# Hybrid decoder layer on one core: the second parts of the first feed-forward, all by seven products

## The chip, the cores and the metric

The kernel runs on one core of a Trainium2 chip, as one program. The metric is the device time of one execution in microseconds. The kernel before took 1702.88 us, the median of three runs (1699.06 to 1704.96).

## The reference

One layer works on 1024 tokens of width 1024, in float32:

```python
h = modulate(rms_norm(x, ffn1_norm), sh1, sc1)
x = x + 0.5 * g1 * ((silu(h @ w_gate) * (h @ w_up)) @ w_down)      # first feed-forward, D_FF = 2816
h = modulate(rms_norm(x, mix_norm), sh2, sc2)
b, c, v, u = split(h @ w_in)                                       # gated convolution and state-space part
x = x + g2 * (concat(rms_norm(y_conv), rms_norm(y_ssm)) @ w_out)
h = modulate(rms_norm(x, ffn2_norm), sh3, sc3)
x = x + 0.5 * g3 * ((silu(h @ w_gate2) * (h @ w_up2)) @ w_down2)   # second feed-forward
y = rms_norm(x, final_norm)
```

The nine vectors sh, sc and g come from `silu(cond) @ w_mod + b_mod`; each of them has 1024 elements.

## The kernel before

The activations lie transposed: features on the 128 partitions, tokens along the row, in two token halves h of 512. Every product keeps its precision by splitting both operands into a high and a low part: `mm3` (line 306) is three matmuls of 128x128 by 128x512 and one tick of a clock that is counted while the program is built. A weight tile of 128x1024 goes from a raw buffer through a cast on ScalarE (high part) and a subtraction on VectorE (low part) into one of four ring buffers (`Weights.pump`). Where sums of two weight blocks are needed, a DMA from GpSimd's queue adds the second block to the raw buffer.

The 2816 inner features of a feed-forward are 11 groups of 256. The first part of a group is its gate and up projections; the second part multiplies the group's 256 activations with its rows of w_down. `seven` (line 626) and `down7` (line 699) compute a 2x2 block product with seven block products instead of eight, as in Strassen's method in Winograd's form. In `down7` the left operands are the activations A11, A12, A21, A22 of a group (token half by feature half) and their sums S1 to S4. They are stored in DRAM by `Kept` (line 477) and loaded again by `fetch` (line 687) as 128x512 tiles: a DMA on SP's queue, a cast on ScalarE, a subtraction on VectorE. A Kept object made with `all_seven` false stores only the A tiles. The sums are made by `keep_sums` and `keep_last`, with four VectorE instructions for a group.

One call of `down7` does a chunk of four groups in two passes p. A pass takes the products of `SEVEN` in their order (A11, S1, S2, S4, S3, A12, A22), each for two output blocks i of 128, into the PSUM banks B, C and A. ScalarE copies three intermediate results out of PSUM (t1, c1, u2), VectorE adds others to them and updates the residual x. The order of products is so chosen that an accumulation into bank C goes on after its copy c1.

Before, the first feed-forward does groups 1 to 4 and 5 to 8 in two chunks (`fad0`, `fad1`). Groups 0, 9 and 10 are done plainly by `last_parts` (line 1391): for each half of the outputs and each token half, 24 calls of mm3 for each of the three groups, tiles named fald. While the second pass of a chunk runs, the operands of the next are fetched, four after each product.

After the last update of a token half, `after1` (line 1312) adds its squares (ScalarE squares, GpSimd or VectorE adds) and orders the norm by clock ticks: 8 ticks later TensorE sums the squares over partitions (n2ast), 7 ticks later it spreads the root (n2abc), and from then on the eight blocks of the next activations h2 are made, one for each tick or when they are asked for. The next TensorE work, the u products, takes these blocks in order, four weight tiles for each block.

`side2` (line 1297) makes 20 elements of 128 of the modulation vectors in this stage, tiles named wm: each a DMA of 512 KB and one multiply-and-sum of 128x1024 on VectorE. One of them is written out at every fourth tick; what is left is written out when the stage ends (`while clock.side: clock.step()`). In this stage each of them carries an edge that keeps it behind the VectorE instruction written before it.

The tile framework orders the instructions of each engine when the program is built, by the order in which they were written and by its own estimate of when their operands are ready. An instruction that it takes to be ready early can be drawn forward. On the chip each engine then works through its queue in that order.

Of the kernel before, what the change touches and what calls it, by code (L numbers as in the profile page):

```python
# [13 lines left out]
F32 = mybir.dt.float32  # L14
# [3 lines left out]
ALU = mybir.AluOpType  # L18
# [3 lines left out]
P = 128  # L22
# [3 lines left out]
KT = D // P  # L26
# [9 lines left out]

CHUNKS = 2

LAST = ((0, NGRP - 2, NGRP - 1), (NGRP - 2, NGRP - 1))
J = S // TAU  # L40
# [79 lines left out]
class Weights:  # L120
# [25 lines left out]

    def seven(self, b, inner=()):
# [11 lines left out]
        self.order.extend(got[q] for q in (2, 3, 4, 1, 5, 6))  # L159

# [4 lines left out]
    def add(self, r, src):  # L165
        self.G.dma_start(out=r[:], in_=src, accum_op=ALU.add)  # L166

    def load(self, upto):
        while len(self.raws) < min(upto, len(self.srcs)):
            i = len(self.raws)  # L170
            r = self.raw_pool(i).tile([P, 1024], F32, tag="raw", name=f"raw{i}")
            src, more = self.srcs[i]
            self.SP.dma_start(r[:], src)
            if more is not None:
                self.add(r, more)
            self.raws.append(r)
# [6 lines left out]
    def pump(self):  # L183
        while self.slots and len(self.tiles) < len(self.granules):
            i = len(self.tiles)
            j, more = self.granules[i]
            self.load(j + 1)
            src = self.raws[j][:]
# [3 lines left out]
            hi, lo = w[:, 0, :], w[:, 1, :]  # L192
            self.A.copy(hi, src)
# [27 lines left out]
@with_exitstack  # L221
def hymba_layer(ctx: ExitStack, tc, x_d, xt_d, wm1_d, wmod_d, gu1_d, gs1_d, ds1_d, wl1_d, win_d, wout_d, glu_d, gu2_d, gs2_d, wd2_d, ds2_d, wl2_d, cols_d, cond_d, lam_d, bc_d, out_d):
    nc = tc.nc
# [56 lines left out]
    def stream(gu, gs, wd, ds, wl, m):  # L280


        for g in range(m):
            plain([gu[2 * g], gu[2 * g + 1]])
        for g in range(m, NGRP):
            ws.seven(gs[g - m], [wd[:, q, :] for q in range(2)] if g == 1 else ())
        for c in range(CHUNKS):
            for p in range(2):
                ws.seven(ds[c, p])
        plain([wl[i] for i in range(wl.shape[0])])  # L290

    stream(gu1_d, gs1_d, None, ds1_d, wl1_d, SEVEN_FROM[0])
    plain([win_d[i] for i in range(8)] + [glu_d] + [wout_d[i] for i in range(4)])
    stream(gu2_d, gs2_d, wd2_d, ds2_d, wl2_d, SEVEN_FROM[1])
    ws.raw_pool = lambda i: pro if i == 3 else rawp

# [390 lines left out]
    def fetch(kept, left, where, name):  # L687
# [6 lines left out]
        SP.dma_start(whole_, kept.stored(left))  # L694
        A.copy(hi, whole_)
        V.tensor_tensor(out=lo, in0=whole_, in1=hi.bitcast(F32), op=ALU.subtract)
        return hi, lo

    def down7(name, lefts, n_, then=None, first=None):

        for p in range(2):
            bank, t1, c1, u2 = {}, {}, {}, {}

            def update(i, h, half, src):
# [10 lines left out]

            for n, (left, b) in enumerate(SEVEN):
                (w,) = ws.take()
                for i in range(2):
                    opens = (b, i) not in bank
                    if opens:  # L720
                        bank[b, i] = ps(f"{name}_{p}_{i}{b}")
                    for k in range(4):
                        mm3(bank[b, i][:], w, 4 * (k // 2) + 2 * (k % 2) + i, lefts[left][k], opens and k == 0, k == 3, more=not opens)
                    if n == 0:
                        copied(t1, "B", i, "t1")
                    elif n == 1:
                        copied(c1, "C", i, "c1")
                    elif n == 2:
                        copied(u2, "B", i, "u2")
                    elif n == 3:  # L730
                        add(u2, "C", i)
                        update(i, 0, 1, u2[i])
                    elif n == 4:
                        add(c1, "B", i)
                        update(i, 1, 1, c1[i])
                    elif n == 5:
# [144 lines left out]

    kept, afs = {0: kept_for(0, 0 not in LAST[0])}, {}

# [101 lines left out]

    kept.update({g: kept_for(g, g not in LAST[0]) for g in range(1, NGRP)})
    gu_first(1)
# [369 lines left out]
    clock.period = 4.5  # L1357
    lefts = [{left: [] for left, _ in SEVEN} for _ in range(CHUNKS)]
    a_last = [{} for _ in LAST[0]]
# [6 lines left out]
    def fetch_last(left):  # L1366

        if left in ("A11", "A12", "A22"):
            i = ("A11", "A12", "A22").index(left)
            for h in range(2):  # L1370
                for fi in range(2):
                    a_last[i][fi, h] = fetch(kept[LAST[0][i]], f"A{h + 1}{fi + 1}", "A", f"fa{LAST[0][i]}l")

# [11 lines left out]
    down7("fad0", lefts[0], 0, lambda left: fetch_chunk(1, left), lambda left: load_x(range(2), (1, 3)) if left == "A12" else None)  # L1385
    down7("fad1", lefts[1], 0, fetch_last)
    clock.period = 4
    clock.side.append(side2(mod_mov, MODS[2]))
    pools["mixed"] = False

    def last_parts():
        for dh in range(2):
            wd = ws.take(3)
            for h in range(2):
                outs = [ps(f"fald{4 * dh + i}_{h}") for i in range(4)]
                for q, (w, a) in enumerate(zip(wd, a_last)):
                    for fi in range(2):
                        for i, o in enumerate(outs):
                            mm3(o[:], w, 4 * fi + i, a[fi, h], q == fi == 0, q == 2 and fi == 1)
                    if h:  # L1400
                        ws.free()
                for i, o in enumerate(outs):
                    d = 4 * dh + i
                    V.scalar_tensor_tensor(out=x[d][h], in0=o[:], scalar=gate[:, 0, d : d + 1], in1=x[d][h], op0=ALU.mult, op1=ALU.add)
                    after1(d, h)

    last_parts()
    while clock.side:
# [290 lines left out]
    HOMES = dict(A11="B", S2="A", A12="B", S3="A", S1="B", A22="A", S4="A")  # L1699
    lefts = [{left: [] for left in HOMES} for _ in range(CHUNKS)]  # L1700
    a_last = {}
# [77 lines left out]
def _arrays(i):  # L1779
# [7 lines left out]
    for n in (1, 2):  # L1787
# [5 lines left out]
        if n == 2:  # L1793
            a["wd2"] = b[0].transpose(1, 2, 0, 3).reshape(P, 2, 1024)
        b = b[list(LAST[n - 1])].transpose(3, 0, 2, 1, 4).reshape(-1, 2, P, 1024)
        a[f"wl{n}"] = b.transpose(0, 2, 1, 3)

        b = wd.reshape(NGRP, 2, P, 2, 2, 2, P)[1 : 1 + 4 * CHUNKS].reshape(CHUNKS, 2, 2, 2, P, 2, 2, 2, P)
        b = b.transpose(0, 6, 1, 4, 3, 5, 2, 7, 8)

        b = [b[:, :, :, :, q, r].reshape(CHUNKS, 2, 2, P, 512).swapaxes(2, 3).reshape(CHUNKS, 2, P, 1024) for q, r in FOUR]
        a[f"ds{n}"] = np.stack(b, axis=2)
        a[f"gu{n}"] = np.stack([g, u], axis=2).reshape(NF, P, 2, 1024)[: 2 * m]
# [21 lines left out]

_ORDER = ["x", "xt", "wm1", "wmod", "gu1", "gs1", "ds1", "wl1", "win", "wout", "glu", "gu2", "gs2", "wd2", "ds2", "wl2", "cols", "cond", "lam", "bc"]

# [16 lines left out]
```

## Time and profile before

| what | value |
|---|---|
| timed runs, median (range) | 1702.88 us (1699.06 to 1704.96) |
| profiled execution, its own time | 1695.99 us |
| span from the first to the last instruction | 1694.2 us |
| matmuls | 7545 recorded |
| first chunk, passes 1 and 2 | 480.3 to 524.2, to 562.3 us |
| second chunk | 562.3 to 638.5 us |
| plain part of three groups | 638.5 to 705.6 us |
| u products | from 705.6 us |

The profiled execution is one more execution than the timed ones and is faster than each of them; durations are read from it. PE is TensorE, DVE VectorE, ACT ScalarE, POOL GpSimd and SP the engine whose queue issues most of the DMAs. A matmul's recorded duration (389 ns) is longer than the distance between two of them, since they overlap. PEclk is the granted share of TensorE's full clock.

### The profile page before, as it was taken

The page shows a single profiled execution, that of the slowest core. Times are in us where ns is not written, and L with a number is a line of the kernel's source. Part 1 is how long each engine was busy: PE and PEld are TensorE (multiplying, and loading weights), DVE is VectorE, ACT ScalarE, POOL GpSimd, SP SyncE. Part 2 cuts the span into 40 slices and gives each one's busy share as a digit, 9 for nine tenths or more (in the row PEclk, how much of TensorE's full clock was granted, in tenths as well). Part 3 has the DMA queues.
Part 4 walks back from the last instruction along what each step waited for, and adds up shares of the span by engine and source line. Part 5 has one row for each costly group of instructions (what it writes and reads, how often), then busy time and mean ns, then how long its engine had stood idle before and what let it go on. Part 6 is the DMA issues. An engine that isn't in the chain of part 4 may idle for free.

```text
span 1694.2 us, 20669 instructions
## 1 busy us (share of the span) xinstructions
PE 1664.0 (98%) x7545; PEld 1370.0 (81%) x7545; DVE 1063.2 (63%) x1572; ACT 670.3 (40%) x983; POOL 165.2 (10%) x203
## 2 busy tenths in 40 slices
PE   8999999999999999999999999999999999999997
PEld 5887878788878888788888778888888888888887
DVE  7976676776566767735666847856555655454454
ACT  7526333333454432332214416434444444322234
POOL 1001000001001102200000121000001001000003
PEclk9999999999999999999999999999999999999999
DMA  9557897887887768235753323557787777989812
GB/s 361 177 164 187 227 265 213 219 210 200 276 275 202 209 177 291 73 101 161 209 156 113 100 99 143 132 136 222 237 234 204 221 219 219 321 272 343 255 60 100
DMA packets 128552, 338.11 MB, mean 200 GB/s; under 512 B 22337, under 2 KB 37953, under 8 KB 127426
## 3 DMA queue, kind: packets, MB, share of 16 engines
q1 hardware_dynamic: 112898, 280.16, 47.7%
q0 software_dynamic: 15552, 56.63, 19.3%
q8 instruction: 59, 0.97, 0.2%
q14 instruction: 43, 0.35, 0.1%
HBM read 252.32 MB, written 76.02 MB: 194 GB/s over the span
## 4 chain that ended last, share of the span: by engine, by line
PE 80%; DVE 8%; DMA 7%; ACT 2%; issue 1%; SPq 1%; POOL 0%; DVEq 0%; POOLq 0%; ACTq 0%
PE fald L111 4%; DMA wm<-in_wmod 3%; PE p L111 3%; PE fbd_1B L111 3%; PE fbd_0B L111 3%; PE fb10d L111 2%; PE fad_0B L111 2%; PE fad_1B L111 2%; PE wo L111 2%; PE b L111 2%; PE u L111 2%; PE fad_1C L111 1%; DMA swx<-X 1%; PE fbd_1C L111 1%; PE fbd_0C L111 1%
## 5 line engine op out<-in xcount | busy, mean ns | idle before, releaser
L111 DVE TENSOR_TENSOR w<-raw,w 128x1024 fp32r<-128x1024 f32 x239 | 292.5, 1226 | 248.3 <-ACT w L111 237.2
L111 ACT CAST w<-raw 128x1024 fp32r<-128x1024 f32 x239 | 250.9, 1051 | 305.0 <-DMA raw<-in_ds 59.4
L166 POOL DMA_DIRECT2D raw<-in_gs x76 | 66.7, 878 | 753.5 <-DVE w L111 425.9
L111 DVE CUSTOM_DVE_ANT_0 wm<-wm,cact 128x1024 f32<-128x1024 f32 x56 | 75.7, 1374 | 38.6 <-DMA wm<-in_wmod 38.6
L166 POOL DMA_DIRECT2D raw<-in_ds x32 | 28.0, 875 | 284.4 <-DVE w L111 162.5
L111 PE MATMUL p<-h,w 128*128 128x512 f32 x192 | 49.4, 407 | 1.7 <-ACT h L111 1.5
L111 PE MATMUL wo<-oa,w 128*128 128x512 f32 x192 | 46.7, 399 | 2.2 <-ACT w L111 2.2
L111 PE MATMUL wo<-ob,w 128*128 128x512 f32 x192 | 45.7, 392 | 1.1 <-ACT ob L111 0.6
L111 PE MATMUL v<-h,w 128*128 128x512 f32 x192 | 46.0, 393 | 0.0
L111 PE MATMUL c<-h,w 128*128 128x512 f32 x192 | 46.0, 393 | 0.0
L111 PEld LDWEIGHTS wo<-oa,w 128*128 128x128 f32 x192 | 36.9, 193 | 10.5 <-ACT w L111 2.6
L111 PE MATMUL b<-h,w 128*128 128x512 f32 x192 | 45.1, 392 | 0.0
L111 PE MATMUL u<-h,w 128*128 128x512 f32 x192 | 44.7, 391 | 0.2 <-DVE h L111 0.2
L111 PEld LDWEIGHTS p<-h,w 128*128 128x128 f32 x192 | 35.7, 192 | 9.9 <-ACT h L111 2.0
L111 PEld LDWEIGHTS wo<-ob,w 128*128 128x128 f32 x192 | 35.7, 188 | 9.3 <-ACT ob L111 1.0
L111 PEld LDWEIGHTS u<-h,w 128*128 128x128 f32 x192 | 35.7, 188 | 8.3 <-DVE h L111 0.6
L111 PEld LDWEIGHTS b<-h,w 128*128 128x128 f32 x192 | 35.7, 188 | 7.3
L111 PEld LDWEIGHTS v<-h,w 128*128 128x128 f32 x192 | 35.5, 188 | 7.1
L111 PEld LDWEIGHTS c<-h,w 128*128 128x128 f32 x192 | 35.5, 188 | 7.0
L111 DVE SCALAR_TENSOR_TENSOR x<-fb10d,gate,x 128x512 f32<-128x512 f32 (+1 forms) x20 | 12.9, 643 | 24.4 <-PE fb10d L111 24.3
L111 PE MATMUL fb10d<-fb9lA,w 128*128 128x512 f32 (+1 forms) x120 | 25.6, 347 | 0.0
L111 DVE TENSOR_TENSOR X<-co,X 128x512 f32<-128x512 f32 x8 | 5.5, 693 | 31.5 <-DMA swx<-X 24.7
(1503 smaller groups left out, 3868.5 us busy)
## 6 DMA issues: line engine op xcount, KB each, us to landing
raw<-in_gs SPq DMA_DIRECT2D x76, 512.0 KB, 4.8
raw<-in_gs POOLq DMA_DIRECT2D x76, 512.0 KB, 6.4
wm<-in_wmod SPq DMA_DIRECT2D x56, 512.0 KB, 6.6
raw<-in_ds SPq DMA_DIRECT2D x32, 512.0 KB, 4.9
raw<-in_ds POOLq DMA_DIRECT2D x32, 512.0 KB, 7.6
mw<-in_wm SPq DMA_DIRECT2D x8, 1024.0 KB, 8.3
raw<-in_win SPq DMA_DIRECT2D x16, 512.0 KB, 4.3
raw<-in_gu SPq DMA_DIRECT2D x12, 512.0 KB, 9.8
```

Of the source, the lines that this page charges most:

```text
L111: r = getattr(self.engine, name)(*args, **kw)
L166: self.G.dma_start(out=r[:], in_=src, accum_op=ALU.add)
```

## The change

The chunks of the first feed-forward become three: groups 1 to 4, groups 0, 8 and 9, and groups 5, 6, 7 and 10. Nothing is left for a plain part. Groups 0, 9 and 10 keep their sums like the others. `down7` takes as many left operands as a chunk has groups, and the weight tiles of the chunk of three are 768 wide. In the last pass the product A12 comes before S3, and A22 gets a bank of its own: x is updated from S3's bank first and from A22's after it. The vectors of `side2` begin with the last pass. `fetch` now only issues the load; its cast and subtraction are written after the following product's loads, and those of the last product after the second product of the next chunk.

```diff
-CHUNKS = 2
-LAST = ((0, NGRP - 2, NGRP - 1), (NGRP - 2, NGRP - 1))
+CHUNKS = ((1, 2, 3, 4), (0, 8, 9), (5, 6, 7, 10)), ((1, 2, 3, 4), (5, 6, 7, 8))
+LAST = (), (NGRP - 2, NGRP - 1)
...
-        A.copy(hi, whole_)
-        V.tensor_tensor(out=lo, in0=whole_, in1=hi.bitcast(F32), op=ALU.subtract)
+        def split():
+            A.copy(hi, whole_)
+            V.tensor_tensor(out=lo, in0=whole_, in1=hi.bitcast(F32), op=ALU.subtract)
+        coming.append(split)
         return hi, lo
...
+    def settle(n=None):
+        for _ in range(len(coming) if n is None else n):
+            coming.popleft()()
+    ENDING = [SEVEN[n] for n in (0, 1, 2, 3, 5, 4)] + [("A22", "A")]
...
-    def down7(name, lefts, n_, then=None, first=None):
+    def down7(name, lefts, n_, then=None, first=None, after=None, begin=None):
         for p in range(2):
+            if p and begin is not None:
+                begin()
+            ending = after is not None and p == 1
...
+                if after is not None and done:
+                    after(d, h)
...
-            for n, (left, b) in enumerate(SEVEN):
+            for n, (left, b) in enumerate(ENDING if ending else SEVEN):
...
-                    opens = (b, i) not in bank
+                    opens = (b, i) not in bank or left == "A22" and b == "A"
...
-                    for k in range(4):
+                    m = len(lefts[left])
+                    for k in range(m):
...
                         update(i, 1, 1, c1[i])
+                        if ending:
+                            update(i, 1, 0, bank["B", i], False)
...
                     else:
-                        update(i, 1, 0, bank["B", i])
+                        update(i, 1, 0, bank[b, i])
                 ws.free()
+                if p == 0 and n == 1:
+                    settle()
...
-    kept, afs = {0: kept_for(0, 0 not in LAST[0])}, {}
+    kept, afs = {0: kept_for(0)}, {}
...
-    kept.update({g: kept_for(g, g not in LAST[0]) for g in range(1, NGRP)})
+    kept.update({g: kept_for(g) for g in range(1, NGRP)})
...
     def after1(d, h):
-        n2[h].add(x[d][h], beside=d < 6)
-        if d == KT - 1:
+        n2[h].add(x[d][h], beside=n2[h].count < 6)
+        if n2[h].count == KT:
             norm_into(act2, h, n2[h], 1, "h2")
...
     def fetch_chunk(c, left, name="fa"):
-        for g in range(1 + 4 * c, 5 + 4 * c):
+        had = len(coming)
+        for g in CHUNKS[name == "fb"][c]:
             lefts[c][left].append(fetch(kept[g], left, HOMES[left], f"{name}{g}l"))
+        settle(had)
...
-    down7("fad1", lefts[1], 0, fetch_last)
-    clock.period = 4
-    clock.side.append(side2(mod_mov, MODS[2]))
-    pools["mixed"] = False
-    def last_parts():
...
-    last_parts()
+    down7("fad1", lefts[1], 0, lambda left: fetch_chunk(2, left))
+    def mods_begin():
+        clock.period = 4
+        clock.side.append(side2(mod_mov, MODS[2]))
+        pools["mixed"] = False
+    down7("fad2", lefts[2], 0, after=after1, begin=mods_begin)
     while clock.side:
         clock.step()
```

The weights w_down of the first feed-forward are laid out on the host as blocks for the three chunks (`ds10`, `ds11`, `ds12`) in place of `ds1` and `wl1`. The second feed-forward keeps its two chunks and its plain part; its kept operands are stored already split, so that `fetch` of them is a load alone, as before.

## Rows read from the trace of the kernel before

**Rows 1.** The page, part 1: engine, busy us, share of the span, instructions.

```profile
PE 1664.0 (98%) x7545; PEld 1370.0 (81%) x7545; DVE 1063.2 (63%) x1572; ACT 670.3 (40%) x983; POOL 165.2 (10%) x203
```

**Rows 2.** Windows by stage: us; PE, PEld, DVE, ACT, POOL busy; PEclk; DMA share; GB/s.

```profile
480.30:524.20 43.90, 40.53 (x169) 32.34 (x168) 31.54 (x42) 20.91 (x32) 3.52 (x4) 0.96 0.80 225
524.20:562.30 38.10, 38.10 (x170) 31.56 (x169) 26.43 (x37) 22.70 (x36) 3.52 (x4) 1.00 0.85 255
600.40:638.50 38.10, 38.10 (x169) 31.56 (x169) 23.02 (x29) 15.06 (x21) 0.88 (x1) 1.00 0.64 192
638.50:705.60 67.10, 67.10 (x305) 55.82 (x305) 52.33 (x74) 15.54 (x22) 15.59 (x9) 1.00 0.58 209
```

**Rows 3.** The chain of waits, 480 to 563 us: start, us, what.

```profile
480.27 2.72 PE fad_0B L111 x12
...
493.81 8.31 DMA fa7lA<-kept7X
503.30 4.61 PE fad_1C L111 x12
...
524.24 2.72 PE fad_0B L111 x12
...
562.32 2.72 PE fad_0B L111 x12
```

**Rows 4.** Timeline of ACT, 499 to 503 us: start, us, instruction, idle before and releaser.

```profile
499.91 0.62 ACT L111 CAST fa4lA<-fa4lA 128x512 fp32r<-128x512 f32 x1 [2.62 <-DMA fa4lA<-kept4X]
...
502.14 0.62 ACT L111 CAST fa7lA<-fa7lA 128x512 fp32r<-128x512 f32 x1
502.67 0.58 ACT L111 COPY fad_1c<-fad_1C 128x512 f32<-128x512 f32 x1
```

**Rows 5.** Groups of DVE instructions by form, 480 to 640 us: busy us, mean ns.

```profile
L111 DVE SCALAR_TENSOR_TENSOR x<-fad_0u,minus,x 128x512 f32<-128x512 f32 x4 | 3.0, 751 | 0.1
...
L111 DVE TENSOR_TENSOR fa8lS<-fa8lS 128x512 fp32r<-128x512 f32 x4 | 2.8, 690 | 0.3 <-ACT fa8lS L111 0.2
...
L111 DVE TENSOR_TENSOR fad_0t<-fad_0t,fad_0A 128x512 f32<-128x512 f32 x4 | 2.7, 682 | 0.1
```

**Rows 6.** Waits of PE, whole span: the longest one for DVE in seven products.

```profile
PE fa6gB L111 <- DVE fa6gc L111: 1.0, 1, 1.0
```

**Rows 7.** Groups of DVE instructions by form, 638 to 705.6 us.

```profile
L111 DVE CUSTOM_DVE_ANT_0 wm<-wm,cact 128x1024 f32<-128x1024 f32 x20 | 28.7, 1470 | 7.4 <-DMA wm<-in_wmod 7.4
...
L111 DVE TENSOR_TENSOR w<-raw,w 128x1024 fp32r<-128x1024 f32 x6 | 7.3, 1220 | 2.6 <-ACT w L111 2.6
L111 DVE SCALAR_TENSOR_TENSOR h2t<-x,scl,n2abc 128x512 f32<-128x512 f32 x5 | 3.5, 743 | 2.9 <-PE n2abc L111 2.9
...
L111 DVE TENSOR_TENSOR n2aq<-n2aq,n2aq 128x512 f32<-128x512 f32 x2 | 1.4, 692 | 1.6 <-POOL n2aq L348 1.5
```

**Rows 8.** Timeline of DVE, 638 to 730 us.

```profile
642.94 1.23 DVE L111 CUSTOM_DVE_ANT_0 wm<-wm,cact 128x1024 f32<-128x1024 f32 x1 [1.54 <-DMA wm<-in_wmod]
...
644.09 0.75 DVE L111 SCALAR_TENSOR_TENSOR x<-fad_1B,gate,x 128x512 f32<-128x512 f32 x1
...
663.69 1.22 DVE L111 CUSTOM_DVE_ANT_0 wm<-wm,cact 128x1024 f32<-128x1024 f32 x1
...
674.05 2.31 DVE L111 CUSTOM_DVE_ANT_0 wm<-wm,cact 128x1024 f32<-128x1024 f32 x1
...
702.64 2.07 DVE L111 SCALAR_TENSOR_TENSOR h<-h2t,mods,h 128x512 fp32r<-128x512 f32 x3
```

**Rows 9.** Timeline of POOL, 638 to 730 us.

```profile
673.24 6.50 POOL L348 TENSOR_TENSOR n2bq<-n2bq,n2bq 128x512 f32<-128x512 f32 x3 [12.49 <-ACT n2bq L111]
686.99 2.67 POOL L348 TENSOR_TENSOR n2aq<-n2aq,n2aq 128x512 f32<-128x512 f32 x2 [7.25 <-ACT n2aq L111]
```

**Rows 10.** Timeline of PE, 685 to 730 us.

```profile
698.43 1.05 PE L111 MATMUL n2abc<-ident,n2arb 128*128 128x128 f32 x8
...
705.46 3.11 PE L111 MATMUL u<-h,w 128*128 128x512 f32 x13
```

More of the change, by code (lines that the diff above doesn't have):

```diff
@@ L145, in plain, with seven @@
         self.order.append(self.granule(self.source(src)))
-    def seven(self, b, inner=()):
+    def seven(self, b, inner=(), last=False):
         b11, b12, b22, b21 = (b[q] for q in range(4))
@@ L158, in seven @@
         got.append(self.granule(y))
-        self.order.extend(got[q] for q in (2, 3, 4, 1, 5, 6))
+        self.order.extend(got[q] for q in ((2, 3, 4, 5, 1, 6) if last else (2, 3, 4, 1, 5, 6)))
     def open(self, pool, n):
@@ L165, in add @@
     def add(self, r, src):
-        self.G.dma_start(out=r[:], in_=src, accum_op=ALU.add)
+        self.G.dma_start(out=r, in_=src, accum_op=ALU.add)
     def load(self, upto):
@@ L191, in pump @@
             w = pool.tile([P, 2, 1024], F32R, tag="w", name=f"w{i}")
-            hi, lo = w[:, 0, :], w[:, 1, :]
+            hi, lo = (w[:, q, : src.shape[-1]] for q in range(2))
             self.A.copy(hi, src)
@@ L286, in stream @@
             ws.seven(gs[g - m], [wd[:, q, :] for q in range(2)] if g == 1 else ())
-        for c in range(CHUNKS):
+        for d in ds:
             for p in range(2):
-                ws.seven(ds[c, p])
-        plain([wl[i] for i in range(wl.shape[0])])
-    stream(gu1_d, gs1_d, None, ds1_d, wl1_d, SEVEN_FROM[0])
+                ws.seven(d[p], last=wl is None and p == 1 and d is ds[-1])
+        if wl is not None:
+            plain([wl[i] for i in range(wl.shape[0])])
+    stream(gu1_d, gs1_d, None, (ds10_d, ds11_d, ds12_d), None, SEVEN_FROM[0])
     plain([win_d[i] for i in range(8)] + [glu_d] + [wout_d[i] for i in range(4)])
-    stream(gu2_d, gs2_d, wd2_d, ds2_d, wl2_d, SEVEN_FROM[1])
+    stream(gu2_d, gs2_d, wd2_d, (ds20_d, ds21_d), wl2_d, SEVEN_FROM[1])
     ws.raw_pool = lambda i: pro if i == 3 else rawp
@@ L1357, in hymba_layer @@
     clock.period = 4.5
-    lefts = [{left: [] for left, _ in SEVEN} for _ in range(CHUNKS)]
-    a_last = [{} for _ in LAST[0]]
+    lefts = [{left: [] for left, _ in SEVEN} for _ in CHUNKS[0]]
     HOMES = dict(A11="A", S2="B", A12="A", S3="B", S1="B", A22="A", S4="A")
     def fetch_chunk(c, left, name="fa"):
-        for g in range(1 + 4 * c, 5 + 4 * c):
+        had = len(coming)
+        for g in CHUNKS[name == "fb"][c]:
             lefts[c][left].append(fetch(kept[g], left, HOMES[left], f"{name}{g}l"))
[L1366 to L1372, printed above, removed]
+        settle(had)
     for g in range(SEVEN_FROM[0], NGRP):
@@ L1385, in hymba_layer @@
     down7("fad0", lefts[0], 0, lambda left: fetch_chunk(1, left), lambda left: load_x(range(2), (1, 3)) if left == "A12" else None)
-    down7("fad1", lefts[1], 0, fetch_last)
-    clock.period = 4
-    clock.side.append(side2(mod_mov, MODS[2]))
-    pools["mixed"] = False
-    def last_parts():
[L1392 to L1405, printed above, removed]
-    last_parts()
+    down7("fad1", lefts[1], 0, lambda left: fetch_chunk(2, left))
[4 more added lines that the diff above has]
+    down7("fad2", lefts[2], 0, after=after1, begin=mods_begin)
     while clock.side:
@@ L1699, in hymba_layer @@
     HOMES = dict(A11="B", S2="A", A12="B", S3="A", S1="B", A22="A", S4="A")
-    lefts = [{left: [] for left in HOMES} for _ in range(CHUNKS)]
+    lefts = [{left: [] for left in HOMES} for _ in CHUNKS[1]]
     a_last = {}
@@ L1794, in _arrays @@
             a["wd2"] = b[0].transpose(1, 2, 0, 3).reshape(P, 2, 1024)
[L1795 to L1802, printed above, removed]
+            b = b[list(LAST[n - 1])].transpose(3, 0, 2, 1, 4).reshape(-1, 2, P, 1024)
+            a[f"wl{n}"] = b.transpose(0, 2, 1, 3)
+        for c, groups in enumerate(CHUNKS[n - 1]):
+            b = wd.reshape(NGRP, 2, P, 2, 2, 2, P)[list(groups)]
+            b = [b[:, q, :, r].transpose(2, 1, 0, 3, 4).reshape(2, P, -1) for q, r in FOUR]
+            a[f"ds{n}{c}"] = np.stack(b, axis=1)
         a[f"gu{n}"] = np.stack([g, u], axis=2).reshape(NF, P, 2, 1024)[: 2 * m]
```

26 lines of the change are left out of this document (14 added, 12 removed).

## The prediction

> **What bounds the kernel now.** I read the page's first part first: TensorE is busy over 98% of the span, VectorE 63% [rows 1]. So what counts is the number of matmuls, and the places where TensorE waits. Then the windows by stage [rows 2]: three of the four stages shown before the u products have TensorE busy throughout; only the first pass of the first chunk (480 to 524) has a hole, with a granted clock of 0.96. The reader is to see the last columns there too: the DMA share was 0.80 to 0.85 while left operands were fetched, and VectorE was busy 52.33 of 67.10 us in the plain stage that the change removes. Third the chain of waits [rows 3]: twelve matmuls take 2.72 us where nothing stalls, so one takes 0.227. A pass of seven products (14 x 12 matmuls) takes 38.08 us, as from 524.24 to 562.32, but the first one took 43.97 (480.27 to 524.24). The 5.89 us are a wait for ScalarE's copy fad_1c, and the half clock behind it: the twelve matmuls at 503.30 took 4.61 us. Last ScalarE's order in that place [rows 4]: the copy stood behind casts of fetched operands, each waiting for its DMA (fa4lA at 499.91, fa7lA's landing 8.31 us after its issue).
>
> **The change part by part.** All sums are against the profiled execution, 1695.99 us (span 1694.2 and 1.8 around it). The median of the timed runs, 1702.88, is 6.9 above it; I add the change to the median.
>
> *Matmuls.* The plain part of three groups has 2 output halves x 2 token halves x 3 groups x 2 x 4 x 3 = 288 matmuls. Seven products of three groups have 2 passes x 7 x 2 x 3 x 3 = 252. The other two chunks keep 336 each. 36 fewer at 0.227 are **-8.2 us**, all on TensorE, which is the bound.
>
> *Fetched operands split one product later.* In the best case all 5.89 us of the first pass go; in the worst none, if ScalarE still gets a cast ahead of the copy (the order is fixed when the program is built, and casts have been drawn forward before: fa7lA belongs to the next chunk and yet ran at 502.14). The next chunk's first casts can hardly stand there any more, since two more kept tiles of group 10 hold the pool's slots; fa4lA's, which began at 499.91, still can, and would leave about 2.9 us. I take the middle of all 5.9 and 3.0: **-4.4**. If the cover goes, what is late next is the weight split on VectorE, which follows the same queue.
>
> *Three more groups keep their sums.* 12 joins of 128x512 on VectorE at about 0.69 (by the splits of the same size [rows 5]), 8.3 us in all, and 6 more stores of 512 KB, beside the first groups and around group 10. In such groups TensorE waited for VectorE at most 1.0 us at a time [rows 6]; I cost them at nothing. If the cover is gone, one group's four joins are 2.8 us. The stores of groups 9 and 10 (2 MB) fall on the fullest stretch of the queues, and can do no more than keep the wait above, which is in its bounds.
>
> *The chunk of three.* Its passes last 126 x 0.227 = 28.6 us, and the second one fetches the next chunk: 28 splits at 0.69, 7 weight splits (estimate 0.92 each, three quarters of 1.22 [rows 7]), 6 additions at 0.68, 8 updates at 0.75 [rows 5]: 35.8 us of VectorE in 28.6. If all splits are done there, 7.2 us are lost; if the 7 or so that find free slots go into the first pass, and the last 4 into the next chunk, about none. Before, the same 28 splits beside 38.1 us of products needed 26.43 and nothing waited [rows 2]. I take **+1.5**. DMA: 7.3 MB of fetches and 3.1 of weights in such a pass, 364 GB/s if nothing is drawn forward, over the 255 of rows 2; that is the same case.
>
> *The end of the third chunk.* Here lies the doubt. The plain part gave 96 groups of three matmuls and so 24 turns for the 20 modulation vectors; the second pass of the third chunk has 56 and so 14 turns. Six vectors are left over, and are written right behind the last product, ahead of the third and later blocks of the next activations (the first two come by the clock before them). I count what VectorE has to do from the first half of the S4 product on, until the third block of activations is ready: 6 additions 4.1; 10 updates 7.5; 4 additions of squares 2.8; 8 + 6 vectors at 1.22, 17.1; 4 weight splits 4.9; three blocks at 2 x 0.743, 4.5 [rows 5, 7]. GpSimd adds squares beside it: a vector then takes 2.31 instead of 1.22 [rows 8, 9], 4 x 1.09 = 4.4. Sum 45.3; neighbours overlap by 7% (three blocks in 2.07, not 2.23 [rows 8]): 42.1. TensorE from there: half a product 2.72, three products 16.3, the sums and the spread of the norm 2 x 1.05 [rows 10], two blocks of u 5.4: 26.6. So up to 15.5 us of waiting, if VectorE takes all in the written order. At the other end, if vectors give way, only the latency of the norm remains: before, the first block came 4.9 us after the spread began (698.43 to 703.3 [rows 8, 10]) and was hidden by nine groups of three matmuls; now one such group and the spread itself hide 1.7, which leaves 3.2. Which end? Vectors do not give way: at 642.94 one that had waited ran ahead of an x update whose products had ended by 638.5 [rows 2, 8]. But they also run early where VectorE has time, and in A11, S1 and S2 it has: 16.3 us less 6 vectors and 3 weight splits, 11.0, leaves 5.3. 15.5 less 5.3 is 10.2, and once the half clock, 1.9 as in rows 3: **+12.1**. Queued behind a late vector are the updates of x, the squares, the norm and so TensorE's first u product.
>
> The Trainium skill ("SBUF — State Buffer", section "Who interferes with whom") says that a VectorE instruction with two SBUF inputs and a GpSimd instruction that reads SBUF exclude each other, the later one waiting out the whole of the other. By that rule each of the four additions would cost VectorE its own undisturbed length, 1.33 (two in 2.67 [rows 9]), 5.3 us in place of 4.4, and the waiting would be 0.9 longer; the trace's 1.09 is lower, and I keep it.
>
> Sum: -8.2 - 4.4 + 1.5 + 12.1 = **+1.0**, that is 1703.9 us.
>
> **The rivals.**
> 1. *Vectors hidden.* The end costs only 3.2, the wait goes whole, the chunk of three is covered: -8.2 - 5.9 + 3.2 = -10.9, 1692.0. For it: the vectors can be delayed without harm, as nothing needs their results in this stage, and VectorE idled 7.4 us on their DMAs before [rows 7], so a fuller queue may lose less than counted. Against: 642.94.
> 2. *VectorE as the bound of the end* (slower). Place: from the S4 product of the last pass to the third u block. Written order throughout, two waits, each followed by half clock: 15.5 + 3.8 = 19.3; -8.2 - 4.4 + 1.5 + 19.3 = +8.2, 1711.1. It decides for slower by over 5.1 us from an end wait of 16.2 on. For it: the count above leaves out the small steps of the norm. Against: VectorE's 5.3 us to spare before.
> 3. *The later split does nothing*, since the order is set by when loads are thought to land and not by where they are written: -8.2 + 1.5 + 12.1 = +5.4, 1708.3.
>
> **How the numbers follow.** About 0.3% (5.1 us) can be told from no change here. My forecast (its own range 1699 to 1709) has 0.34, rival 1 0.28, rival 2 0.26, rival 3 0.12, half of it on either side of that line. So faster 0.28, same 0.34 + 0.06 = 0.40, slower 0.26 + 0.06 = 0.32. The range 1691 to 1716 takes in rival 2 with 5 us more and all but the lower part of rival 1.
>
> **What would show it.** Right: 924 matmuls in the first feed-forward's second parts, a first pass of chunk one of about 38 to 40 us, and waits of u on h, or on the norm, of 8 to 15 us in all. Wrong: a first u block within 4 us of the last product and no wait at the third; ScalarE's copy still behind a cast; or waits inside the chunk of three above 3 us. The prediction fails if the vectors left over run behind the blocks of h, or if VectorE is not full in the last pass.

## The result and the profile after

The changed kernel takes 1706.28 us (median of 20 runs, 1701.38 to 1713.25); the kernel before, run beside it, 1700.97 (20 runs, 1698.63 to 1705.86). The ratio is 1.0028, 95% interval [1.0017, 1.0039]: a little slower, and clear of one. That is 5.3 us more by the medians and 4.8 by the ratio, so it lies at the very edge of the 0.3% (5.1 us) that the prediction took as no change. The time lies in the predicted range, 2.4 us above the predicted 1703.9. Of that nearness 1.9 us are luck: the prediction added its +1.0 to a median of 1702.88, and the 20 runs of before gave 1700.97. The change itself came out 4.3 us above its forecast.

The profiled execution of the changed kernel took 1709.98 us, 3.7 above its median; that of before, 1695.99, lies 5.0 below the median of its 20 runs. So the two traces differ by 14.0 us where the kernels differ by 5.3, and I compare stretches, each from the first matmul of one stage to the first of another (PE's timeline), with a second profiled execution of either kernel beside the first (experiments 11 and 12):

| us | fad0 begins | first pass of chunk one | last chunk's first pass | last pass to product c | fad0 to c | c to the end |
|---|---|---|---|---|---|---|
| before | 480.11 | 43.97 | | 153.10 | 273.23 | 940.9 |
| before, again | 485.75 | 44.13 | | 153.10 | 273.39 | 942.6 |
| after | 484.81 | 42.62 | 38.63 | 101.44 | 277.89 | 945.1 |
| after, again | 483.95 | 42.52 | 39.12 | 100.94 | 277.78 | 945.3 |

For before "last pass to c" holds the last pass, the plain part (288 matmuls x 0.2267 = 65.3) and the products u; for after the last pass and u. Taken without the plain part, before has 87.8 there and after 101.2. Of 85.0 us TensorE could not be relieved: a pass 38.08, u 192 x 0.2267 = 43.5, sums and spreads of the norm 3.4. I call the rest the **loss at the end**: 2.8 before; 16.4 and 15.9 after.

The page of after, part 1 (the columns are those of [rows 1]):

```profile
PE 1663.6 (97%) x7509; PEld 1368.0 (80%) x7509; DVE 1086.1 (64%) x1615; ACT 686.9 (40%) x1012; POOL 172.0 (10%) x211
```

36 matmuls fewer than in [rows 1]; VectorE has 43 instructions more. Windows of after by stage (columns as in [rows 2]): first pass, second pass of chunk one; chunk of three; the last chunk's first pass; its second pass with the spread of the norm; from there to the third block of u; the rest of u. The last line is the stretch from VectorE's addition fad_0u, which closes the first half of the S4 product, to the end of the third block of h.

```profile
484.80:527.40 42.60, 39.99 (x169) 32.57 (x168) 31.99 (x44) 20.48 (x31) 3.53 (x4) 0.96 0.92 271
527.40:565.50 38.10, 38.10 (x169) 31.53 (x168) 26.47 (x38) 22.73 (x37) 3.53 (x4) 1.00 0.83 249
565.50:622.60 57.10, 57.10 (x253) 47.30 (x252) 39.52 (x55) 25.60 (x41) 6.17 (x7) 1.00 0.75 196
622.60:661.30 38.70, 38.45 (x170) 31.49 (x169) 30.11 (x37) 18.53 (x28) 11.11 (x9) 1.00 0.76 177
661.30:703.30 42.00, 40.50 (x185) 33.09 (x183) 34.27 (x50) 16.08 (x22) 9.79 (x8) 1.00 0.89 306
703.30:722.10 18.80, 9.64 (x36) 7.15 (x36) 18.80 (x31) 4.15 (x7) 2.11 (x1) 0.77 0.50 169
722.10:762.70 40.60, 40.59 (x172) 33.52 (x173) 21.98 (x32) 14.72 (x22) 1.02 (x1) 0.94 0.22 61
...
682.20:722.10 39.90, 29.24 (x129) 22.92 (x127) 38.31 (x61) 11.74 (x16) 7.68 (x5) 0.89 0.74 264
```

The sixth line is the place of the cost: VectorE is busy 18.80 of 18.80 us, TensorE 9.64, and the granted clock is 0.77 there. Before, the same vectors lay beside 67.10 us of products that never waited (last line of [rows 2]). The chunk of three, in the third line, has TensorE busy throughout, at two passes of 28.56 us.

What TensorE waited for from the last pass to c in after (us in total, times, longest):

```profile
PE u L111 <- ACT h L111: 6.2, 1, 6.2
PE u L111 <- DVE h L111: 2.9, 1, 2.9
PE n2ast L111 <- DVE n2aq L111: 1.1, 1, 1.1
PE n2abc L111 <- DVE n2arb L111: 0.4, 1, 0.4
```

10.6 us of waits. Of the other 5.8 us of the loss, 4.5 are the half clock behind the waits: by PE's timeline 22 matmuls of this stretch stand 0.43 us apart in place of 0.227. The remaining 1.3 lie in smaller delays. VectorE's timeline of after in that place, where the blocks of h that u needs stand among vectors (wm):

```profile
703.32 1.22 DVE L111 TENSOR_TENSOR w<-raw,w 128x1024 fp32r<-128x1024 f32 x1
704.45 2.28 DVE L111 CUSTOM_DVE_ANT_0 wm<-wm,cact 128x1024 f32<-128x1024 f32 x1
...
709.25 1.21 DVE L111 CUSTOM_DVE_ANT_0 wm<-wm,cact 128x1024 f32<-128x1024 f32 x1
...
710.39 0.74 DVE L111 SCALAR_TENSOR_TENSOR h<-h2t,mods,h 128x512 fp32r<-128x512 f32 x1
...
713.45 0.74 DVE L111 SCALAR_TENSOR_TENSOR h<-h2t,mods,h 128x512 fp32r<-128x512 f32 x1
714.12 1.21 DVE L111 CUSTOM_DVE_ANT_0 wm<-wm,cact 128x1024 f32<-128x1024 f32 x1
...
721.31 0.74 DVE L111 SCALAR_TENSOR_TENSOR h<-h2t,mods,h 128x512 fp32r<-128x512 f32 x1
```

From the spread of the norm, TensorE's last work ahead of u (done by 703.3; the last product by 701.8), to the third block of h (721.31) seven vectors run, five of them between the second and the third block; the two waits of u end at the first block (709.5, by ScalarE's) and at this third one (722.1). In [rows 8] three blocks ran in one piece of 2.07 us.

The first pass of chunk one, which answers to [rows 3, 4]: chain of waits of after, then ScalarE's timeline.

```profile
495.41 7.34 DMA fa4lA<-kept4X
503.30 0.59 ACT fad_0c L111
503.93 4.32 PE fad_0C L111 x12
```

```profile
502.77 0.62 ACT L111 CAST fa4lA<-fa4lA 128x512 fp32r<-128x512 f32 x1 [2.00 <-DMA fa4lA<-kept4X]
503.30 0.58 ACT L111 COPY fad_0c<-fad_0C 128x512 f32<-128x512 f32 x1
```

The copy still stands behind the cast of fa4lA, which waits for its DMA; it is only another copy, fad_0c, with a shorter wait and the half clock (4.32 for 2.72) after it.

### The profile page after: what moved, and what is told of

Its sections match the earlier page's. It is cut to its first block, busy times and chain, and to the rows that moved or that the text cites. A ratio compares the mean times of both kernels' runs of the same rounds, so it can differ in the third digit from the quotient of the medians.

```text
span 1707.8 us, 20750 instructions
## 1 busy us (share of the span) xinstructions
PE 1663.6 (97%) x7509; PEld 1368.0 (80%) x7509; DVE 1086.1 (64%) x1615; ACT 686.9 (40%) x1012; POOL 172.0 (10%) x211
## 4 chain that ended last, share of the span: by engine, by line
PE 71%; DVE 13%; DMA 10%; ACT 3%; issue 2%; SPq 1%; POOL 0%; DVEq 0%; POOLq 0%; ACTq 0%
DMA wm<-in_wmod 3%; PE fbd_1B L111 3%; PE fbd_0B L111 3%; PE fb10d L111 2%; PE fad_0B L111 2%; PE fad_1B L111 2%; PE u L111 2%; DVE w L111 2%; PE wo L111 2%; DMA swx<-X 2%; DVE wm L111 2%; PE b L111 2%; PE fad_0C L111 1%; PE fad_1C L111 1%; PE fbd_1C L111 1%
## 5 line engine op out<-in xcount | busy, mean ns | idle before, releaser
L111 DVE TENSOR_TENSOR w<-raw,w 128x1024 fp32r<-128x1024 f32 (+1 forms) x247 | 299.2, 1214 | 246.9 <-ACT w L111 242.7
L111 ACT CAST w<-raw 128x1024 fp32r<-128x1024 f32 (+1 forms) x247 | 256.2, 1039 | 283.1 <-DMA raw<-in_ds 86.2
L166 POOL DMA_DIRECT2D raw<-in_ds x40 | 35.1, 878 | 316.0 <-DVE w L111 140.5
L111 PE MATMUL u<-h,w 128*128 128x512 f32 x192 | 49.1, 417 | 9.2 <-ACT h L111 6.2
```

The lines of the kernel that those rows point to most:

```text
L111: r = getattr(self.engine, name)(*args, **kw)
L166: self.G.dma_start(out=r, in_=src, accum_op=ALU.add)
```

## The experiments

The numbers of a kernel are its median against that of before in the same series. Beside it stand its stretches, as in the table above.

**1. Six vectors put off.** The last pass gets 14 vectors, for its 14 turns; the other six go to the stage of the output product.

```
-    MODS = (12, 12, 20, 12)
+    MODS = (12, 12, 14, 18)
```

> The changed kernel, but side2 makes 14 elements of the modulation vectors in the last pass and 6 more in the stage after the state-space part, instead of 20 and 12: nothing is left over behind the last product. Theory 1 (VectorE's queue: what stands in it before the first blocks of h sets the end): six fewer vectors of 1.14 us ahead of the blocks; the waits of u on h (9.2 us in the changed kernel, with 2.4 of half clock behind) fall to 2 to 5 us, and the time falls by 5 to 9 us against the changed kernel (about 1698 to 1701 if the changed kernel is at 1706), less 0 to 3 for the six vectors where they go. Theory 2 (the norm's own latency: only two groups of three matmuls stand between it and u): the waits stay above 8 us, the time moves by less than 2.

1705.17 us, ratio 1.0016 [1.0004, 1.0028]. The loss at the end falls from 16.4 to 10.5 and the second wait of u is gone:

```profile
PE u L111 <- ACT h L111: 6.2, 1, 6.2
PE n2ast L111 <- DVE n2aq L111: 0.7, 1, 0.7
...
```

So the six left over made the wait for the third block, about 1 us a vector; the first wait, 6.2, is not theirs. Theory 1 has the direction right, but 6.2 us of waits of u remain where it said 2 to 5, and the time gains only 1.1 on the changed kernel's median, less than its runs differ. By the stretches fad0 to c took 273.1 us, 4.8 less than in the changed kernel, and the six vectors behind cost 0.4 (c to the end 945.6). That most of this is not seen in the medians, no run explains. The chunk of three, with the same code, lost 2.5 us here (59.6 for its two passes in place of 57.1).

**2. All 20 vectors begun one pass sooner,** with the last chunk's first pass.

```
-            if p and begin is not None:
+            if p == 0 and begin is not None:
```

> The changed kernel, but the vectors begin with the first pass of the third chunk: 28 turns for 20. Theory 1: none is left over, and those in the last pass fall from 14 to 6, so 14 x 1.2 = 17 us of VectorE leave the end, where 14 us were lost: waits of u on h of at most 3 us, the time 10 to 13 us below the changed kernel (about 1694). Theory 3 (rival: the pool of 20 slots holds 16 left operands and two sums in the first pass, so only two vectors can be in flight and each later one comes at the DMA's pace of 7 to 8 us for two; VectorE, which takes its queue in order, blocks on them, and x updates and weight splits come late): waits of TensorE inside the first pass of 5 us or more, and a time within 4 us of the changed kernel or above it.

1711.67 us, ratio 1.0051 [1.0035, 1.0067]. No vector was left after the last product, and yet the loss at the end was 18.3. TensorE's waits in the last chunk, and VectorE's timeline:

```profile
PE n2ast L111 <- DVE n2aq L111: 4.5, 1, 4.5
PE fad_0C L111 <- DVE w L111: 3.3, 3, 2.8
PE u L111 <- ACT h L111: 3.2, 1, 3.2
```

```profile
692.08 1.23 DVE L111 CUSTOM_DVE_ANT_0 wm<-wm,cact 128x1024 f32<-128x1024 f32 x1 [1.76 <-DMA wm<-in_wmod]
...
693.23 1.22 DVE L111 TENSOR_TENSOR w<-raw,w 128x1024 fp32r<-128x1024 f32 x1
694.37 0.68 DVE L111 TENSOR_TENSOR fad_0u<-fad_0u,fad_0C 128x512 f32<-128x512 f32 x1
```

The addition fad_0u closes the first half of the S4 product, whose matmuls ended at 687.8; it ran at 694.37, behind the last vector, which had waited 1.76 us for its data. Five such waits in this chunk take 5.2 us. So in this trace the addition, and behind it the x updates, the squares and the norm, are late by the vectors in front of them, though none is left over. Theory 3 holds in kind and not in place: the last chunk's first pass lost 1.6 us (39.6), the end 18.3.

**3. Operands split at once,** in the changed kernel: the later split undone.

```
-        coming.append(split)
+        split()
```

> The changed kernel, but a fetched operand is split where it is loaded, as before. Theory 1 of this part (what orders ScalarE's queue is when the planner takes a load to be there; where the split is written matters little): the first pass of the first chunk takes 41 to 45 us as in both kernels (43.97 before, 42.8 in the changed one), the time moves by less than 2 us. Rival (the later place is what holds the casts back): the first pass takes 46 us or more, or the chunk of three stalls by 3 us or more, and the time is 3 to 8 us above the changed kernel.

1715.68 us, ratio 1.0082 [1.0066, 1.0099]. By the medians the later split is worth 9.4 us here (8.6 if either kernel is set against before in its own series), and the rival by which it does nothing is refuted. The first pass of chunk one takes 49.63 (42.62), the last chunk's first pass 42.6 (38.63); TensorE waits in the former:

```profile
PE fad_0C L111 <- DVE w L111: 6.2, 2, 4.4
```

That is the place that the prediction named for a lost cover (the weight split on VectorE); but 49.63 is also 5.7 more than before, which splits at once too. Experiments 5 and 10 ask for the reason.

**4. A shorter turn,** so that the 20 vectors fit into the last pass.

```
-        clock.period = 4
+        clock.period = 2.75
```

> The changed kernel, but a vector is written at every 2.75th tick of the last pass instead of every fourth: all 20 are written inside it, none behind the last product, and VectorE's amount of work is the same. If the amount decides (VectorE full from the S4 product on): waits in the norm and for the blocks of h of the same sum, and the time within 3 us of the changed kernel. If the place of the left-over six decides: those six run in the light products A11, S1 and S2, the wait at the later u blocks goes, and the time is 5 to 8 us lower.

1713.30 us, ratio 1.0066 [1.0043, 1.0089]; loss at the end 22.8:

```profile
PE n2ast L111 <- DVE scl L111: 6.2, 1, 6.2
PE u L111 <- ACT h L111: 5.3, 1, 5.3
PE n2abc L111 <- DVE n2arb L111: 4.5, 1, 4.5
```

All 20 are written inside the pass, two still run behind the last product, and the norm itself now waits for VectorE. So it is not only the place of the left-over six that decides: moving the vectors forward in this pass made it 7.0 us worse, which neither forecast had.

**5. The sums alone,** in the kernel before: groups 0, 9 and 10 keep theirs, made and stored and used by nothing.

```
-    kept, afs = {0: kept_for(0, 0 not in LAST[0])}, {}
+    kept, afs = {0: kept_for(0)}, {}
...
-    kept.update({g: kept_for(g, g not in LAST[0]) for g in range(1, NGRP)})
+    kept.update({g: kept_for(g) for g in range(1, NGRP)})
```

> The kernel before, and in it the three groups that its last parts take (0, 9 and 10) also get the sums of a seven-product group, which are stored and then used by nothing. So it adds only the stores' preparation of the change. Theory A (the 4.7 us by which the changed kernel reaches its first second part later come of these sums: they lengthen VectorE's and GpSimd's queues in the gate and up products): the first product of fad0 comes 3 to 6 us later than the 480.1 us of before, and the time is 3 to 6 us above it (about 1705). Theory B, as the prediction had it (the sums cost nothing, the 4.7 us are a chance of the order that the planner gave the changed kernel): fad0 within 1 us of 480.1 and the time within 0.1 per cent of before.

1707.14 us, ratio 1.0043 [1.0030, 1.0056]: 5.8 us for a term that the prediction had put at nothing. fad0 came at 485.48 as theory A said, but so it did without any sums (experiment 11), and the cost is elsewhere, where neither theory had it: the first pass takes 49.99 us in place of 44. Chain of waits of this kernel (start, us, what):

```profile
494.07 0.69 DVE fa10X L111
...
495.20 7.47 DMA fa1lA<-kept1X
...
502.70 0.63 ACT fa1lA L111
...
504.04 1.20 DVE fa10Z L111 x2
505.24 0.61 DVE fa10W L111
...
510.61 1.15 DVE w L111
...
511.80 4.63 PE fad_0C L111 x10
```

Group 10 is the last one before the second parts. Its sums (fa10X, Z, W) run inside the first pass, on VectorE between the splits of fetched operands, and the weight split that fad_0C needs comes at the end of that row. The last of the three tiles named fa1lA is late here too: its cast began 17.2 us after fad0 (502.70 less 485.48), in the second execution of before 9.5 (495.28 less 485.75). SP's queue, which issues its load, shows why; first the kernel before, then this one:

```profile
480.06 0.32 SPq L111 DMA_DIRECT2D fa1lA<-kept1X  x1
487.67 0.32 SPq L111 DMA_DIRECT2D kept10X<-fa10X  x1
```

```profile
494.78 0.33 SPq L111 DMA_DIRECT2D kept10X<-fa10X  x1
495.20 0.38 SPq L111 DMA_DIRECT2D fa1lA<-kept1X  x1
```

Before, the load was issued as fad0 began, ahead of the store of fa10X. Here it stands behind this store, which waits for VectorE, and goes out 9.7 us after fad0; in experiment 3, which has the same sums and splits at once too, 9.8 after it. In experiment 10, without the sums of groups 9 and 10, it goes out 0.4 ahead of fad0. In experiment 6, with the later split and without the sums, it stands behind the store too, 4.9 after fad0, and there the pass is at its shortest: the late load by itself does not make the cost. Why the two changed places when the program was built, no run shows.

**6. The later split alone,** in the kernel before: the lines of the diff on coming and settle, for its last parts as well.

```
-        A.copy(hi, whole_)
-        V.tensor_tensor(out=lo, in0=whole_, in1=hi.bitcast(F32), op=ALU.subtract)
+        coming.append(split)
...
+        settle(had)
```

> The kernel before with the later split alone: every fetched left operand (those of the last parts too) is copied and subtracted one product after its load; chunks, products and vectors as before. Theory A (the prediction's term: the stall of 5.9 us in the first second part is ScalarE waiting for loads in front of the copy of fad_0c): its first pass takes 39 to 42 us in place of 43.97 and the time falls by 2 to 5 us. Theory B (what splitting at once cost in the changed kernel, 9.4 us, was mostly its third chunk, whose first pass took 42.6 us then against 38.6): here there is no third chunk, the first pass falls by under 2 us as in the changed kernel (43.97 to 42.62), and the time by 0 to 2 us. Theory C (it does nothing): within 0.1 per cent of before.

1699.70 us, ratio 0.9993 [0.9981, 1.0006]. The first pass falls to 40.57, as theory A had it, 3.5 under the 44.05 of before's two executions; the time by 1.7, which is not told from nothing. TensorE still waits 1.3 us for ScalarE's copy:

```profile
PE fad_1C L111 <- ACT fad_1c L111: 1.3, 1, 1.3
```

**7. No vector in the last pass:** 8 more in the first groups, 12 more behind.

```
-    MODS = (12, 12, 20, 12)
+    MODS = (20, 12, 0, 24)
```

> The changed kernel with none of the 20 modulation vectors in the last pass: 8 more stand in the first gate and up groups (20 in place of 12 there) and 12 more in the stage of the output product (24 in place of 12). Theory A (the vectors in VectorE's queue make the end long: 16.4 us lost from the last pass to the product c in the changed kernel): the loss falls to the bare length of the norm, 3 to 6 us; the 12 vectors behind cost nothing or up to 3, the 8 ahead up to 3; the time is 1693 to 1700, under both kernels. Theory B (it is the norm itself, all of whose sums now come after the last products, so that vectors or none it stays): the loss stays over 11 us and the time within 3 us of the changed kernel or above it.

1717.46 us, ratio 1.0094 [1.0078, 1.0110]. The loss at the end is 7.7, between the two theories, and the moved vectors cost more than they saved: in the first groups one product waited 8.6 us for weights (fad0 at 493.35),

```profile
PE fa2gC L111 <- DVE w L111: 6.0, 1, 6.0
PE fa2gC L111 <- ACT w L111: 2.6, 1, 2.6
```

and c to the end took 954.7, 9.5 more.

**8. Eight vectors in the last pass,** 12 more behind.

```
-    MODS = (12, 12, 20, 12)
+    MODS = (12, 12, 8, 24)
```

> The changed kernel with 8 of the 20 modulation vectors in the last pass and 12 more in the stage of the output product (24 in place of 12). With 14 in the last pass the loss from the last pass to c was 10.5 us against 16.4 with 20, about 1 us a vector. Theory A (that line goes on): the loss is about 5 us, and the time 1700 to 1703 if the 12 vectors behind cost up to 3 us. Theory B (the floor is the norm): the loss stays near 10 us, and with the 12 vectors behind the time is 1704 to 1708.

1707.36 us, ratio 1.0033 [1.0017, 1.0048]. The loss at the end is 3.4: the changed products are then 7.8 us shorter from fad0 to c than before (265.4 against 273.2), about the gain of the 36 matmuls. But c to the end takes 953.4, 8.2 more than in the changed kernel, with waits in the stage that got the vectors:

```profile
PE n3ast L111 <- DVE n3aq L111: 4.1, 1, 4.1
PE wo L111 <- DVE w L111: 3.6, 1, 3.6
```

So theory A holds for the end, and fails for the whole by what it put on the vectors behind (up to 3). That experiment 7, with no vector, lost 4.3 us more at the end than this one with eight shows that the order there has other costs; they were not followed.

**9. The vectors spread** over the chunk of three's second pass and the whole last chunk.

```
-        clock.period = 4
+        clock.period = 6.5
...
-    down7("fad1", lefts[1], 0, lambda left: fetch_chunk(2, left))
+    down7("fad1", lefts[1], 0, lambda left: fetch_chunk(2, left), begin=mods_begin)
...
-    down7("fad2", lefts[2], 0, after=after1, begin=mods_begin)
+    down7("fad2", lefts[2], 0, after=after1)
```

> The changed kernel with the same 20 modulation vectors spread over the second chunk's second pass and the whole third chunk (one in 6.5 steps from there, in place of one in 4 from the last pass on), so that each has its load in time and all stand in front of the last products. Theory A (the end is long by the vectors that stand among its updates, sums and blocks, and a vector that has its data in time costs nothing earlier): the loss from the last pass to c falls from 16.4 us to 3 to 6 us, as with 8 vectors, nothing is put into a later stage, and the time is 1692 to 1698, under both kernels. Theory B (in a second part VectorE stands at each vector until its load is there, as with all 20 in the third chunk, and what is behind it comes late): waits of TensorE for VectorE in the middle passes and a loss at the end of over 10 us; the time is 1704 or more.

1705.93 us, ratio 1.0027 [1.0012, 1.0043], the changed kernel's time. The loss at the end falls by 6.5, to 9.9, but the two passes from 593.34 on take 72.3 in place of 67.2, with these waits:

```profile
PE fad_0B L111 <- DVE fad_0c L111: 2.4, 1, 2.4
PE fad_0C L111 <- DVE w L111: 1.1, 1, 1.1
```

Neither theory alone: the vectors had their data here (VectorE shows no wait for it), and the 14 of them that ran ahead of the last pass cost TensorE 5.1 us in the middle, most of what they no longer cost at the end.

**10. The sums of group 0 alone,** in the kernel before: the first of experiment 5's two edits.

> The kernel before with the sums of a seven-product group for group 0 alone (made, stored, used by nothing), where the run with those of groups 0, 9 and 10 took 5.8 us more and reached fad0 5.4 us later. Theory A (group 0's sums, which fall where VectorE and GpSimd are already late for the groups 2 to 6, make the delay before fad0; those of 9 and 10 lengthen the first second part): fad0 comes 4 to 6 us later than 480.1 us, the first pass takes 44 us as before, the time is 1704 to 1706. Theory B (the sums of 9 and 10 make both): fad0 within 1.5 us of before, time 1700 to 1702.

1700.74 us, ratio 0.9997 [0.9983, 1.0011], first pass 42.02. So group 0's sums cost nothing, and the 5.8 us of experiment 5 come with those of 9 and 10 (which of the two, no run tells), as theory B had it for the time. fad0 began at 487.49, and still the time is that of before: where fad0 begins says little.

**11 and 12. Both kernels again,** unchanged, for their second profiles.

> The kernel before, unchanged, profiled once more. Its first profiled execution, 1695.99 us, lies 5.0 us below the median of its 20 runs. Theory A (what comes before fad0 differs from one execution to the next by several us, whatever the kernel; the 4.7 us by which the changed kernel reached fad0 later are such a difference, and the sums cost nothing there): this time fad0 begins at 482 to 487 us, and the time is near 1701. Theory B (480.1 us is the kernel's own, and the later fad0 of the kernels with added sums is the sums' cost): fad0 begins within 1 us of 480.1 again.

> The changed kernel, unchanged, profiled once more (the first time 1709.98 us, 3.7 above its median). Theory A (the end is long by the vectors in its queue, as worked out): the loss from the last pass to c is 13 to 18 us again (16.4 the first time), with vectors among the blocks of h and two waits of the product u. Theory B (the 16.4 us are a bad execution, and the kernel's own loss is nearer to the 10.5 us of the run with 14 vectors): the loss is 9 to 12 us. In both the first pass of the first chunk takes 41 to 43 us, and each pass of the chunk of three under 30.

1703.49 and 1709.14 us, one run each. fad0 of before began at 485.75, not 480.11; its first pass and its end repeat to 0.2 us. The window of before's first pass, second execution:

```profile
485.80:529.90 44.10, 40.86 (x170) 32.34 (x169) 31.77 (x43) 21.31 (x33) 3.52 (x4) 0.96 0.79 214
```

The loss at the end of after was 15.9 this time, with nearly the same two waits of u:

```profile
PE u L111 <- ACT h L111: 6.2, 1, 6.2
...
PE u L111 <- DVE h L111: 3.0, 1, 3.0
```

Theory A in both. In all kernels but that of experiment 7, fad0 began between 480.1 and 487.5; two executions of one kernel lie 5.6 apart there, so these differences tell little of the kernels. c to the end took 940.9 to 945.6 but for experiments 7 and 8. The traces of before and after differ there by 4.2 and 2.7; experiments 3 and 4, with the changed kernel's code behind c, took 941.9 and 942.0, so whether any of that is the change's is open.

## Why the prediction was right, and where it was not

The time lies in the range, and the largest cost has the mechanism that was forecast. That it counts as no change is a close call, at the edge of the 0.3%, and part of the nearness is luck, as said above. From fad0 to c, where the change lies, the kernels differ by +4.5 us (277.8 against 273.3), and the terms by stretches add up to it: -8.2 - 1.5 + 0.8 + 13.4 = +4.5; the medians differ by +5.3.

- *Matmuls, -8.2:* right. 36 fewer, and two passes of 28.56 us; in experiment 8, where the other terms about cancel, the stretch from fad0 to c is 7.8 shorter than before.
- *Later split, -4.4, and three more groups' sums at nothing:* here the prediction failed. Two sentences of it failed: "In such groups TensorE waited for VectorE at most 1.0 us at a time [rows 6]; I cost them at nothing", which looked at the products of the groups alone, and that the last groups' stores "can do no more than keep the wait above". The 1.0 us, besides, is one execution's: in the second one of before TensorE waited 2.9 us in group 5 and 2.4 in group 4. The sums of the last groups fall into the first pass, where splits and weight splits wait in VectorE's row: +5.9 there with everything split at once (44.1 to 49.99). The later split then takes 7.0 off the same pass (49.63 to 42.62), more than the 5.9 that the prediction set as its whole worth. The two together are -1.5, not -4.4; alone, in experiment 6, the later split gave -3.5, near its term, so it is the sums that were sized wrong. The bound for a lost cover (2.8 for one group's four joins) was too small: it counted the joins and not the load that goes out later behind a store. How much of the 5.9 is the load's and how much the joins', no run took apart. The sign that it named for this failure, ScalarE's copy still behind a cast, is there.
- *Chunk of three, +1.5:* right in size. Both its passes run without a wait; +0.5 and +1.0 show in the pass after it, behind waits of 0.3 and 0.5 us for a weight split. In experiment 1 the chunk itself lost 2.5, so the term is not the same from kernel to kernel.
- *End of the third chunk, +12.1:* right in mechanism, 1.3 short: 13.6 and 13.1. It had six vectors ahead of the third block; seven ran after the last product. It counted 42.1 us of VectorE from fad_0u's addition to the third block; in the trace of after that is 682.1 to 722.1, 40.0, and VectorE is busy for 38.31 of 39.90 us there. The waits of u and the norm are 10.6, within its 8 to 15. The half clock cost more than its 1.9: the 24 matmuls behind the first wait took 7.66 us (709.53 to 717.19), 2.2 over 24 x 0.227, and another wait followed.
- *Vectors hidden* (rival 1): refuted for this kernel; but with only eight vectors in the last pass (experiment 8) the end costs 0.6 more than before (a loss of 3.4 against 2.8), even less than its 3.2.
- *VectorE as the bound of the end* (rival 2): it is the forecast's own mechanism at a higher price. VectorE is full from the last product to the third block, but 34.27 of 42.00 us in the pass ahead of it, and the price, 13.4, stayed under the 16.2 from which the prediction would have called the kernel slower.
- *The later split does nothing* (rival 3): refuted by experiment 3, 9.4 us.
- *The signs*: of those for right, 924 matmuls and waits of 8 to 15 us came, and the first pass of 38 to 40 us did not (42.6). Of those for wrong, the copy behind a cast came, and, taken by its words, a VectorE that is not full in the last pass: the pass has 34.27 of 42.00 us. Full it was from the S4 product on, the stretch that the forecast adds up.

What lay under all of it: the plain part was the cover of the 20 vectors. At the end they cost about 1 us each (16.4, 10.5 and 3.4 us lost with 20, 14 and 8), in the middle 5.1 for 14 (experiment 9), behind 8.2 for 12 (experiment 8), though 0.4 for six (experiment 1). So most of the expected gain was paid out again wherever they stood, and no version tried beats the kernel before by more than can be measured. The nearest is the later split alone, 0.9993 [0.9981, 1.0006].

Of the addition on GpSimd against vectors, the trace of after has one case in the end, at 704.45 in the timeline above, and this line of GpSimd:

```profile
703.55 2.11 POOL L350 TENSOR_TENSOR n2bq<-n2bq,n2bq 128x512 f32<-128x512 f32 x1 [1.93 <-ACT n2bq L111]
```

The addition began while a weight split ran (703.32 to 704.54) and took 2.11, where one by itself takes 1.3 (two in 2.67 [rows 9]): it ended 1.12 after the split. The vector began while the addition ran and ended 1.07 after it, 2.28 in all instead of 1.21. That each ran after the other agrees with the Trainium skill ("SBUF — State Buffer", section "Who interferes with whom"). The prediction had read 1.09 a meeting from the row and four meetings. In the trace the three additions before this one (684.32, 688.48 and 699.07) each began while a vector ran; they ended late, after 1.49 to 1.55, and the vector did not. So only one of the four delayed a vector; one more did at the start of the pass, and the two took 2.28 and 2.33, the other 18 vectors 1.21 to 1.23.

## What to carry to other kernels

Before a stage with spare time on a second engine is taken out, list what was put there because of that time, and price it where it would go next; here 36 matmuls were saved, and 20 vectors lost their place. Cost added work in the stretch where its engine's queue is fullest, not where it is written: the sums of group 0 were free, and those of groups 9 and 10 cost 6 us at the border to the next stage. Look there at what stands behind a store in the queue that issues the loads. And profile the kernel before twice: the changed stretches repeat to half a us, the time up to them does not.

## Not expected of the hardware

Behind a wait of 6.2 us the granted clock was 0.77 over the 18.80 us that hold both waits of u and 0.94 over the 40.60 after them, so at the lower of its two levels, 1.2 GHz, for part of both. And the same program reached the same matmul at 480.11 in one execution and at 485.75 in the next. Group 6 already began at 277.86 and 284.03, after waits for VectorE of 2.4 and 2.9 us in groups 4 and 5 that the first execution does not have.
